# A pooling mixer on one Trainium2 core: the band in fp32 on its nonzero columns, seven warm-ups, one weight split on GpSimd, the scale in two transfers

## The chip, the cores and the metric

The kernel runs on one core of one Trainium2 chip. The metric is device microseconds (us) for one execution of the whole program. The engines are named as in the profile: PE (TensorE matmul) and PEld (its weight load), DVE (VectorE), ACT (ScalarE), POOL (GpSimd), SP (SyncE, which only issues transfers here). L351 is line 351 of the kernel before; L333 and the like, where said so, are lines of the changed kernel.

## The reference

Two decoder layers on x of 512 tokens by 1024 features in fp32. Layer 0 mixes tokens by a causal pooling, layer 1 by differential attention; after each mixer comes a LayerNorm on ALPHA * x + mixer(x), then a SwiGLU block with a second LayerNorm. Only the first mixer matters here. The features fall into four groups of 256; group g replaces each token by the mean of the last w tokens (w = 2, 4, 8, 16) less the token itself, multiplies by its own 256 x 256 weight and scales the result:

```python
pooled.append((hi - lo) / cnt)            # mean over the window, fewer tokens at the start
mixed = jnp.einsum('bsgc,gcd->bsgd', pooled - xg, w)
return mixed.reshape(B, S, D) * scale
```

As a matrix, "mean less itself" is a band: token t takes 1/w from each of tokens t-w+1 to t, less 1 at t. For a block of 128 tokens that act as sources only 144 columns of the band are nonzero: its own 128 tokens and the first 16 of the next block.

## The kernel before

All products that need fp32 accuracy are made of three products of a cheaper type, fp32r: each operand is split into a high part (rounded by ACT, L105) and a low part (the rest, subtracted by DVE, L106), and high x high, high x low and low x high are added (`mm3`, L123 to L125). Weights come from one tensor in pieces of 128 x 1024 (`fetch`, L95, issued by SP into five buffers `raw`), and are split by `ready` (L106). The order of instructions on each engine is the order in which the code is written; nothing is rescheduled. Each engine runs its own list in that order and waits where an operand isn't there.

The pooling stage is the head of the program. SP issues, in order, blocks 0 and 1 of x (`res`, L82), the first pooling weight `raw0`, the scale (L252, one row of 1024 values copied to all 128 partitions), block 2, the second pooling weight `raw1`, block 3, and gate weights from `raw2` on. Meanwhile POOL makes index ramps and the identity and fills the empty columns of the band tiles `fh` and `bh` with zeros (L276 to L278), DVE makes the band (L293 to L299), and ACT rounds a 16 x 16 corner `d0` for the first tokens, whose mean has fewer terms. PE runs 22 fp32 products of zeros (L312, `WARM`), whose result is used by nobody.

Each 128 x 512 half of a block of x is then split (`split_x`, eight times in all: blocks 0 and 1 ahead of the first pooled half, block 2 and block 3 later). `low` (L351 to L356) and `high` (L365, L366) multiply the split x with the band over 256 columns, zeros included, into eight PSUM banks `pool0_g` (tokens 0 to 255) and `pool1_g` (tokens 256 to 511). `scale_weights` multiplies a pooling weight by the scale on DVE (L325); `pool_weights` splits it (ACT L334, DVE L337); `split_pooled` splits a pooled bank; `mixed(s, d)` multiplies block s of the pooled tokens with the weights of two groups (24 products for both halves d). Then, block by block, DVE adds the result to x (`residual`, L154), takes statistics (L161, L167, L169), POOL takes the root (L170), DVE normalizes (L179), PE transposes (L206), ACT applies gain and shift (L225), and ACT and DVE split the result into `xt`, the input of the SwiGLU block. That block begins with tokens 0 to 255 alone: its first product, g<-xt,w2h, needs `xt` of blocks 0 and 1 and the split gate weight w2. Blocks 2 and 3 are turned between its first products. `w2` and `w3` are the first two gate weights (`raw2`, `raw3`); the low part of w2 is subtracted on DVE behind `spread_of(0, 0)`.

Of the kernel before, what the change touches and what calls it, by code (L numbers as in the profile page):

```python
# [11 lines left out]
F32 = mybir.dt.float32  # L12
F32R = mybir.dt.float32r
# [28 lines left out]
WARM = 22  # L42
# [10 lines left out]
def trunk(ctx, tc, x, wall, pscale, lam_p, subln, table, lng, lnb, first, onehot, out):  # L53
# [190 lines left out]
    with tc.tile_pool(name="pool", bufs=1) as pp:  # L244
# [4 lines left out]
        load_x(1)  # L249
        fetch(1)  # L250
        scale = pp.tile([P, D], F32, name="scale")
        nc.sync.dma_start(out=scale, in_=pscale.broadcast_to([P, D]))  # L252
        load_x(2)
        fetch(2)
# [3 lines left out]
        fh = pp.tile([P, 4, 256], F32R, name="fh")  # L258
        fl = pp.tile([P, 4, 256], F32R, name="fl")
        bh = pp.tile([P, 4, 512], F32R, name="bh")  # L260
        still = pp.tile([P, P], F32, name="still")
        nc.vector.memset(still, 0.0)
        nc.scalar.copy(
            fl.rearrange("p g (a t) -> p (g a) t", a=2), still.unsqueeze(1).to_broadcast([P, 8, P])
        )
# [10 lines left out]
        nc.gpsimd.memset(fh[:, :, 144:].bitcast(F32), 0.0)  # L276
        nc.gpsimd.memset(bh[:, :, 0:P].bitcast(F32), 0.0)
        nc.gpsimd.memset(bh[:, :, P + 144 :].bitcast(F32), 0.0)  # L278
# [12 lines left out]
        near = pp.tile([P, 4, 144], F32, name="near")  # L291
        for g, w in enumerate(WINDOWS):
            nc.vector.tensor_scalar(  # L293
                near[:, g, :], after, scalar1=float(w), scalar2=1.0 / w, op0=ALU.is_lt, op1=ALU.mult
            )
        own = ident.unsqueeze(1).to_broadcast([P, 4, P])
        for t in (fh[:, :, 0:144], bh[:, :, P : P + 144]):
            nc.vector.tensor_copy(t[:, :, P:], near[:, :, P:])
            nc.vector.tensor_tensor(t[:, :, :P], near[:, :, :P], own, op=ALU.subtract)  # L299
        xnh, xnl = (  # L300
            xt[:, i].rearrange("p a k s -> p (a k s)").rearrange("p (s d) -> p s d", s=SB)
            for i in range(2)
        )

        def split_x(s, d, low=None):
            c = slice(d * 512, (d + 1) * 512)
            split(xnh[:, s, c], xnl[:, s, c], res[:, s, c], low=low)
# [5 lines left out]
        split(fh[:16, :, 0:16], fl[:16, :, 0:16], d0)  # L313
        split_x(0, 0)
        split_x(0, 1)
        split_x(1, 0)
        split_x(1, 1)
# [25 lines left out]
        def xk(t, s, k):  # L343
            return t[:, s, k * P : (k + 1) * P]

        def low(t, ks):
            for k in ks:
                g = k // 2
                o = made[0, g][:, (k % 2) * 256 : (k % 2 + 1) * 256]
                if t == 0:  # L350
                    mm(o, xk(xnh, 0, k), fh[:, g, :], start=k % 2 == 0, stop=False)  # L351
                    mm(o, xk(xnh, 0, k), fl[:, g, :], start=False, stop=False)
                    mm(o, xk(xnl, 0, k), fh[:, g, :], start=False, stop=False)
                else:
                    mm(o, xk(xnh, 1, k), bh[:, g, 0:256], start=False, stop=False)
                    mm(o, xk(xnl, 1, k), bh[:, g, 0:256], start=False, stop=k % 2 == 1)  # L356

        def high(blocks, ks):
            for s in blocks:
                c = (3 - s) * P  # L360
                for k in ks:
                    g = k // 2
                    o = made[1, g][:, (k % 2) * 256 : (k % 2 + 1) * 256]
                    b = bh[:, g, c : c + 256]
                    mm(o, xk(xnh, s, k), b, start=s == 1 and k % 2 == 0, stop=False)  # L365
                    mm(o, xk(xnl, s, k), b, start=False, stop=s == 3 and k % 2 == 1)  # L366
# [1053 lines left out]
```

## Time and profile before

| | us |
|---|---|
| median of 3 runs (lowest, highest) | 946.09 (945.66, 946.59) |
| the profiled execution | 946.19 |
| its span, first to last instruction | 944.4 |
| PE busy in the span | 932.3 (99%) |
| DVE busy in the span | 823.5 (87%) |
| start of the first gate product, g<-xt,w2h | 36.70 |

The span begins with the first instruction that the profile shows; 1.79 us of the profiled execution lie outside it. A timeline row gives the start, the duration, the engine, the line and the operation, what it writes and reads, and how many such instructions were merged; in brackets stands how long its engine had been idle and what it waited for. A matmul of PE starts before the one ahead of it has drained, so its pace is the distance between starts, not its duration. One fp32 product is two PE instructions (22 warm-ups are 44), one fp32r product is one.

### The profile page before, as it was taken

The numbers are of one execution on the slowest core, as the hardware profiler recorded it, in microseconds if no ns is written. First come the engines' busy times: TensorE is split into PE (matmuls) and PEld (weight loads), VectorE is DVE, ScalarE is ACT, GpSimd is POOL, SyncE is SP. The second block draws the span as 40 slices with busy tenths as digits, with TensorE's granted clock in tenths as the row PEclk, the third lists the DMA queues.
The fourth block names the chain that finished last, engine by engine and source line by source line (L and its number), as shares of the span: only waits on it lengthen the run. The fifth ranks groups of instructions, "written<-read, shape, count | busy, mean of one in ns | idle before, by whom it ended". The sixth has DMA issues, their size and how long they took to land. (4 is left out here: it accounts for less than half of the span.)

```text
span 944.4 us, 16089 instructions
## 1 busy us (share of the span) xinstructions
PE 932.3 (99%) x6293; PEld 858.9 (91%) x6293; DVE 823.5 (87%) x1220; ACT 505.8 (54%) x810; POOL 104.9 (11%) x136
## 2 busy tenths in 40 slices
PE   9999999999999999999999999999999999999996
PEld 9899999999988888988888888899999999988885
DVE  7999999999988798688777676799999999988898
ACT  5664454554564467665556553844455554663550
POOL 2111121110001101000000000211111110001101
PEclk9999999999999999999999999999999999999998
DMA  7288998886878965432232232389998786878962
GB/s 272 70 254 271 300 291 260 253 264 205 259 243 269 357 211 157 148 90 101 67 91 78 67 90 90 100 250 276 277 283 252 246 272 211 257 235 274 360 223 89
DMA packets 73499, 197.40 MB, mean 209 GB/s; under 512 B 6546, under 2 KB 17970, under 8 KB 73424
## 3 DMA queue, kind: packets, MB, share of 16 engines
q1 hardware_dynamic: 33840, 114.44, 36.8%
q0 software_dynamic: 15952, 47.31, 18.5%
q10 hardware_dynamic: 23632, 34.63, 9.9%
q8 instruction: 49, 0.80, 0.3%
q14 instruction: 26, 0.21, 0.1%
HBM read 159.64 MB, written 36.72 MB: 208 GB/s over the span
## 5 line engine op out<-in xcount | busy, mean ns | idle before, releaser
L603 DVE TENSOR_TENSOR raw<-raw,raw 128x1024 f32<-128x1024 f32 x72 | 87.8, 1219 | 0.6
L105 ACT CAST xs<-hid 128x512 fp32r<-128x512 f32 (+1 forms) x60 | 34.7, 582 | 28.5 <-DVE hid L768 28.5
L106 DVE TENSOR_TENSOR xs<-hid,xs 128x512 fp32r<-128x512 f32 (+1 forms) x60 | 38.3, 640 | 7.8 <-ACT xs L105 7.8
L225 ACT ACTIVATE y<-pt,gbT 128x128 f32<-128x128 f32 x92 | 34.6, 456 | 19.3 <-PE pt L206 19.3
L1142 ACT ACTIVATE p<-p,mn 128x128 f32<-128x128 f32 (+3 forms) x64 | 35.4, 554 | 14.9 <-DVE mn L1137 14.9
L699 POOL DMA_DIRECT2D b<-in_wall x24 | 17.9, 793 | 155.4 <-DMA tsum<-b 132.4
L760 POOL DMA_DIRECT2D xs<-ssum x24 | 17.4, 725 | 141.8 <-PE Q L915 119.3
L170 POOL TENSOR_TENSOR rs<-rs,mhalf 128x1 f32<-128x1 f32 x16 | 12.6, 791 | 167.8 <-DVE rs L169 167.8
L875 ACT ACTIVATE sg<-sg 128x512 f32<-128x512 f32 x18 | 11.4, 633 | 33.5 <-DVE sg L866 33.5
L1137 DVE CUSTOM_DVE_ANT_0 p<-s,bias 128x128 f32<-128x128 f32 (+3 forms) x64 | 28.1, 485 | 0.0
L106 POOL TENSOR_TENSOR sql<-sq,sqh 128x512 fp32r<-128x512 f32 x7 | 9.1, 1294 | 165.3 <-ACT sqh L105 165.3
L736 ACT CAST v<-u 128x512 fp32r<-128x512 f32 x22 | 13.7, 621 | 22.1 <-DVE u L734 22.0
L106 DVE TENSOR_TENSOR xt<-y,xt 128x512 fp32r<-128x512 f32 x23 | 15.5, 686 | 11.4 <-ACT xt L105 11.4
L699 POOL DMA_DIRECT2D hid<-in_wall x20 | 14.7, 734 | 95.2 <-DMA tsum<-hid 71.7
L858 ACT COPY hid<-C 128x512 f32<-128x512 f32 x18 | 10.6, 588 | 24.2 <-PE C L847 24.2
L161 DVE BATCH_NORM_STATS2 st<-res 128x6 f32<-128x512 f32 x32 | 22.2, 694 | 1.1
L106 DVE TENSOR_TENSOR heads<-k,heads 128x512 fp32r<-128x512 f32 x8 | 5.5, 691 | 20.2 <-ACT heads L105 20.2
L862 DVE TENSOR_TENSOR hid<-C,hid 128x512 f32<-128x512 f32 x18 | 12.4, 690 | 10.9 <-PE C L847 9.2
L700 POOL DMA_DIRECT2D b<-in_wall x12 | 14.8, 1229 | 57.1 <-DMA b<-in_wall 47.2
L105 ACT CAST heads<-k 128x512 fp32r<-128x512 f32 x8 | 4.7, 588 | 26.3 <-PE k L125 26.3
L1156 DVE SCALAR_TENSOR_TENSOR p<-p,sm,p 128x128 f32<-128x128 f32 (+3 forms) x32 | 17.6, 551 | 1.1
L1132 PE MATMUL s<-heads 64*128 64x256 f32 (+2 forms) x192 | 17.9, 330 | 0.0
(1150 smaller groups left out, 3804.7 us busy)
## 6 DMA issues: line engine op xcount, KB each, us to landing
raw<-in_wall SPq DMA_DIRECT2D x122, 512.0 KB, 4.2
r<-tsum SPq DMA_DIRECT2D x40, 512.0 KB, 4.4
b<-in_wall POOLq DMA_DIRECT2D x36, 512.0 KB, 5.9
hid<-in_wall POOLq DMA_DIRECT2D x30, 512.0 KB, 6.0
r<-in_wall SPq DMA_DIRECT2D x30, 512.0 KB, 5.0
tsum<-b ACTq DMA_DIRECT2D x24, 512.0 KB, 5.1
ssum<-v ACTq DMA_DIRECT2D x22, 512.0 KB, 3.6
tsum<-hid ACTq DMA_DIRECT2D x20, 512.0 KB, 5.0
```

What stands on the lines that cost most here:

```text
L105: nc.scalar.copy(dst_h, src)
L106: (low or nc.vector).tensor_tensor(dst_l, src, dst_h.bitcast(F32), op=ALU.subtract)
L161: nc.vector.bn_stats(stats[n, s][:, d, :], res[:, s, d * 512 : (d + 1) * 512])
L225: nc.scalar.activation(y[:, k, :], src, AF.Identity, bias=b, scale=g)
L603: tt(t, raws[pair[0]], raws[pair[1]], op=ALU.add)
L699: nc.gpsimd.dma_start(out=t[:, j], in_=src[:, j])
L700: nc.gpsimd.dma_start(out=t[:, 0], in_=src[:, :, 1], accum_op=ALU.add)
L760: nc.gpsimd.dma_start(out=t.bitcast(F32), in_=ssum[:, 0 if p == "P7" else 1, :, r, :])
L1132: nc.tensor.matmul(accs[c][:, :wide], a[r, qs], b[r, :wide], start=i == 0, stop=i == 2)
L1137: nc.vector.tensor_tensor_reduce(out=p, in0=accs[c][:, :w], in1=biases[h][:, w - 1 :: -1] if w < S else biases[h][:, ::-1], op0=ALU.add, o ...
L1142: nc.scalar.activation(p, p, AF.Exp, bias=mn[:, q, c : c + 1], scale=-1.0, accum_out=sm[:, q, c : c + 1],)
L1156: nc.vector.scalar_tensor_tensor(p0[:, r], p0[:, r], sm[:, q, 0:1], p1[:, r], op0=ALU.mult, op1=ALU.add)
```

## The change

The band is applied to x as it is, in fp32: `split_x`, `low` and `high` go, and `shares` takes their place. It multiplies a 128 x 128 piece of a block of x with only those columns of the band that are not zero (144, 128 or 16), in one fp32 product each. The tiles `fh`, `fl` and `bh` give way to `band` and `edge` (the band with the corner `d0` for the first block), 144 columns wide, without zero columns to fill. The warm-ups are 7 instead of 22. The scale comes in two transfers of 512 columns, the first ahead of `raw0`, the second behind block 2. The low part of w2 is subtracted on POOL. The code behind it stands in a somewhat other order: the split of the second half of the pooled tokens now follows both residuals of block 1, and the split of w3 is made in one piece.

```diff
-WARM = 22
+WARM = 7
...
+        load_scale(0)
         fetch(1)
-        scale = pp.tile([P, D], F32, name="scale")
-        nc.sync.dma_start(out=scale, in_=pscale.broadcast_to([P, D]))
         load_x(2)
+        load_scale(1)
         fetch(2)
...
-        nc.gpsimd.memset(fh[:, :, 144:].bitcast(F32), 0.0)
-        nc.gpsimd.memset(bh[:, :, 0:P].bitcast(F32), 0.0)
-        nc.gpsimd.memset(bh[:, :, P + 144 :].bitcast(F32), 0.0)
...
+        nc.scalar.copy(edge[:, :, P:], band[:, :, P:])
         own = ident.unsqueeze(1).to_broadcast([P, 4, P])
+        for t in (edge, band):
+            nc.vector.tensor_tensor(t[:, :, :P], band[:, :, :P], own, op=ALU.subtract)
+        nc.scalar.copy(edge[:16, :, 0:16], d0)
...
-        split(fh[:16, :, 0:16], fl[:16, :, 0:16], d0)
-        split_x(0, 0)
-        split_x(0, 1)
-        split_x(1, 0)
-        split_x(1, 1)
...
+        def shares(half, s, source, a, b, o, first=False):
+            for k in range(KB):
                 g = k // 2
+                c = (k % 2) * 256 + o
+                mm(
+                    made[half, g][:, c : c + b - a],
+                    res[:, s, k * P : (k + 1) * P],
+                    source[:, g, a:b],
+                    start=first and k % 2 == 0,
+                    stop=False,
+                    skip_group_check=True,
+                )
...
-        low(0, range(4))
-        low(0, range(4, 8))
-        low(1, range(8))
+        shares(0, 0, edge, 0, 144, 0, True)
+        shares(0, 1, band, 0, P, P)
+        shares(1, 1, band, P, 144, 0, True)
         scale_weights(0)
-        high((1,), range(8))
         pool_weights(0)
         split_pooled(0, 0, 1)
+        shares(1, 2, band, 0, 144, 0)
         mixed(0, 0)
-        split_x(2, 0)
-        split_x(2, 1)
-        high((2,), range(8))
         scale_weights(1)
...
-        split_x(3, 0)
-        split_x(3, 1)
-        summed(0, 0)
...
+        ready(3, nc.gpsimd)
+        mixed(1, 1)
+        shares(1, 3, band, 0, P, P)
+        summed(0, 0, 1)
+        spread_of(0, 0)
...
-        high((3,), range(8))
...
+        summed(1, 0)
+        norm(0, 0)
+        summed(1, 1)
+        spread_of(0, 1)
+        split_pooled(1, 0, 1)
+        norm(0, 1)
```

On DVE, between the split of the pooled bank of group 1 and the first residual, the kernel before has these rows (`pooled` is the split pooled tile, `xt<-res` a split of x, `raw_88` the second pooling weight, `pw1l` its low part, `mix_0` the first product of block 0):

```order
L106 TENSOR_TENSOR pooled<-pool_1_131,pooled 128x2x256 [waits Activation_49]
L106 TENSOR_TENSOR xt<-res,xt 128x512 [waits DMAHW5_49,Activation_49]
L106 TENSOR_TENSOR xt<-res,xt 128x512 [waits Activation_49]
L325 TENSOR_TENSOR raw_88<-raw_88,scale 128x512 [waits DMAHW6_49]
L325 TENSOR_TENSOR raw_88<-raw_88,scale 128x512
L106 TENSOR_TENSOR pooled<-pool_2_132,pooled 128x2x256 [waits Activation_49]
L106 TENSOR_TENSOR pooled<-pool_3_133,pooled 128x2x256 [waits Activation_49]
L337 TENSOR_TENSOR pw1l<-raw_88,pw1h 128x512 [waits Activation_49] x2
L106 TENSOR_TENSOR xt<-res,xt 128x512 [waits DMAHW7_49,Activation_49]
L106 TENSOR_TENSOR xt<-res,xt 128x512 [waits Activation_49]
L154 SCALAR_TENSOR_TENSOR res<-res,mix_0_236 128x512 [waits PE_49]
```

On the same engine at the same place the changed kernel has (`raw_89` is now the second pooling weight, L311 its scaling, L323 its low part):

```order
L106 TENSOR_TENSOR pooled<-pool_1_126,pooled 128x2x256 [waits Activation_49]
L311 TENSOR_TENSOR raw_89<-raw_89,scale 128x512 [waits DMAHW7_49,DMAHW6_49]
L311 TENSOR_TENSOR raw_89<-raw_89,scale 128x512
L106 TENSOR_TENSOR pooled<-pool_2_127,pooled 128x2x256 [waits Activation_49]
L106 TENSOR_TENSOR pooled<-pool_3_128,pooled 128x2x256 [waits Activation_49]
L323 TENSOR_TENSOR pw1l<-raw_89,pw1h 128x512 [waits Activation_49] x2
L106 TENSOR_TENSOR tbl<-tb,tbh 33x8 [waits DMASW2_49,Activation_49]
L154 SCALAR_TENSOR_TENSOR res<-res,mix_0_182 128x512 [waits DMAHW0_49,PE_49]
```

The four splits of x are gone; the scaling now waits for two transfers, its weight and the second half of the scale.

Further down on DVE, from the statistics of block 0 to the split of the second pooled half, the kernel before has (`mv` and `rs` hold mean and inverse root, `w2l` is the low part of the first gate weight, `mix_0_282` and `mix_1_283` the two halves of block 1):

```order
L169 TENSOR_SCALAR rs_0_347<-mv_0_345 128x1 [waits DVE_49]
L106 TENSOR_TENSOR w2l<-raw_91,w2h 128x1024 [waits DMAHW0_49,Activation_49]
L106 TENSOR_TENSOR tbl<-tb,tbh 33x8 [waits DMASW2_49,Activation_49]
L154 SCALAR_TENSOR_TENSOR res<-res,mix_0_282 128x512
L161 BN_STATS st_1_377<-res 128x6 [waits DVE_49]
L179 TENSOR_SCALAR res<-res,mv_0_345,rs_0_347 128x1024 [waits Pool_49]
L106 TENSOR_TENSOR pooled<-pool_0_134,pooled 128x2x256 [waits PE_49,Activation_49]
```

And the changed kernel, from the same row on (`mix_0_208` and `mix_1_209` are block 1):

```order
L169 TENSOR_SCALAR rs_0_281<-mv_0_279 128x1 [waits DVE_49]
L154 SCALAR_TENSOR_TENSOR res<-res,mix_0_208 128x512 [waits DMAHW2_49]
L161 BN_STATS st_1_285<-res 128x6 [waits DVE_49]
L179 TENSOR_SCALAR res<-res,mv_0_279,rs_0_281 128x1024 [waits Pool_49]
L154 SCALAR_TENSOR_TENSOR res<-res,mix_1_209 128x512 [waits PE_49]
L161 BN_STATS st_1_285<-res 128x6 [waits DVE_49]
L167 BN_AGGR mv_1_290<-st_1_285 128x2 [waits DVE_49]
L169 TENSOR_SCALAR rs_1_292<-mv_1_290 128x1 [waits DVE_49]
L106 TENSOR_TENSOR pooled<-pool_0_129,pooled 128x2x256 [waits Activation_49]
```

The low part of w2 has left DVE, and the second residual of block 1 with its statistics now stands ahead of the pooled split instead of behind it.

On POOL the subtraction of w2 is now queued ahead of the roots; the changed kernel's rows from its last transfers of constants on are:

```order
L285 DMA tb<-in_table 32x8 [waits Pool_49]
L287 DMA oh__113<-in_onehot 33x640
L106 TENSOR_TENSOR w2l<-raw_92,w2h 128x1024 [waits DMAHW1_49,Activation_49]
L170 TENSOR_TENSOR rs_0_281<-rs_0_281,mhalf 128x1 [waits DVE_49]
L170 TENSOR_TENSOR rs_1_292<-rs_1_292,mhalf 128x1 [waits DVE_49]
```

In the kernel before, the first root follows `oh_` directly.

72 lines of the change are left out of this document (12 added, 60 removed).

## The prediction

> **What bounds the kernel now.** First the page's shares of busy time, then busy time by stage: the stage of the change ends at 36.70, where the first gate product starts.
>
> ```profile
> PE 932.3 (99%) x6293; PEld 858.9 (91%) x6293; DVE 823.5 (87%) x1220; ACT 505.8 (54%) x810; POOL 104.9 (11%) x136
> core 0: us, PE busy (x) PEld busy (x) DVE busy (x) ACT busy (x) POOL busy (x), PEclk, DMA share, GB/s
> 0.00:36.70 36.70, 33.83 (x250) 33.05 (x250) 31.52 (x60) 23.98 (x45) 7.54 (x20) 0.95 0.56 204
> 36.70:67.00 30.30, 30.30 (x256) 30.30 (x255) 28.68 (x36) 19.71 (x36) 6.55 (x8) 1.00 0.67 191
> ```
>
> From 36.70 on PE never stops, so an earlier start of that product is worth its whole shift, if what feeds PE moves along. Before it, PE's 33.83 us say little: they hold warm-ups and a stretch at half clock. PE's rows show where that stage is held:
>
> ```profile
> 1.06 5.65 PE L312 MATMUL pool<-still 128*128 128x128 f32 x25 [1.06 <-DVE still L262]
> 6.34 2.37 PE L312 MATMUL pool<-still 128*128 128x128 f32 x19
> 8.58 0.36 PE L351 MATMUL pool<-fh,xt 128*128 128x256 f32 x1
> 26.84 1.81 PE L206 MATMUL pt<-ident,res 128*128 128x128 f32 x8 [1.82 <-DVE res L179]
> 28.30 0.56 PE L123 MATMUL mix<-pw0h,pooled 128*128 128x256 f32 x1
> 36.02 0.39 PE L439 MATMUL line<-ohr,tbh 33*8 33x512 f32 x1
> 36.70 0.39 PE L123 MATMUL g<-xt,w2h 128*128 128x256 f32 x1
> ```
>
> PE waits once, 1.82 us for DVE's normalization. DVE is the engine to follow; these are the rows that carry it:
>
> ```profile
> 5.12 2.57 DVE L106 TENSOR_TENSOR xt<-res,xt 128x512 fp32r<-128x512 f32 x4 [0.75 <-ACT xt L105]
> 8.98 1.29 DVE L325 TENSOR_TENSOR raw<-raw,scale 128x512 f32<-128x512 f32 x2 [1.29 <-DMA scale<-in_pscale]
> 13.98 1.28 DVE L106 TENSOR_TENSOR xt<-res,xt 128x512 fp32r<-128x512 f32 x2
> 15.19 1.29 DVE L325 TENSOR_TENSOR raw<-raw,scale 128x512 f32<-128x512 f32 x2
> 18.79 1.28 DVE L106 TENSOR_TENSOR xt<-res,xt 128x512 fp32r<-128x512 f32 x2
> 20.00 0.68 DVE L154 SCALAR_TENSOR_TENSOR res<-res,mix 128x512 f32<-128x512 f32 x1
> 21.59 0.69 DVE L154 SCALAR_TENSOR_TENSOR res<-res,mix 128x512 f32<-128x512 f32 x1 [0.19 <-PE mix L125]
> 23.28 0.15 DVE L169 TENSOR_SCALAR rs<-mv 128x1 f32<-128x1 f32 x1
> 23.36 1.22 DVE L106 TENSOR_TENSOR w2l<-raw,w2h 128x1024 fp32r<-128x1024 f32 x1
> 24.51 0.15 DVE L106 TENSOR_TENSOR tbl<-tb,tbh 33x8 fp32r<-33x8 f32 x1
> 25.90 0.80 DVE L179 TENSOR_SCALAR res<-res,mv,rs 128x1024 f32<-128x1024 f32 x1
> 35.88 0.69 DVE L106 TENSOR_TENSOR xt<-second,xt 128x512 fp32r<-128x512 f32 x1
> ```
>
> A row without a bracket didn't wait. From 13.98 to the last row the only wait shown is 0.19 us; that row, the low part of the last piece of `xt`, ends at 36.57 and the gate product starts at 36.70. That chain is what an edit must shorten; PE's own chain, up to the same point, is nearly as long.
>
> **The change part by part.**
>
> *Warm-ups and the first shares.* The 25 warm-up instructions to 6.34 take 5.28 us, 0.211 each; the 19 behind them 2.24 us, 0.118 each. So the 14 that are left end at about 4.0. The first share needs block 0 of x and the corner; the first cast of before shows when x is there:
>
> ```profile
> 4.47 2.42 ACT L105 CAST xt<-res 128x512 fp32r<-128x512 f32 x4 [0.34 <-DMA res<-in_x]
> L312 PEld LDWEIGHTS pool<-still 128*128 128x128 f32 x44 | 7.6, 273 | 1.1 <-DVE still L262 1.1
> ```
>
> PE's pool work thus starts at 4.45 instead of 8.58. No row has this product on real x; the warm-up is the same form. Priced by it, 144 columns are 16 instructions of 0.211 x 1.125 while slow and 0.118 x 1.125 when fast: shares(0,0) is 2.1 to 3.8, and with the pace doubling near 6.4 as before it ends at about 7.5; shares(0,1) adds 1.9 (9.4). For 16 columns the bounds are an eighth of that (0.24) and all of it (1.9), since the weight load stays whole; I take 1.2, nearer the load (10.6). shares(1,2) ends at 12.7. Fast, the five come to 9.2 us. Before, 88 fp32r products did this; PE's pace from 36.70 on is 256 instructions in 30.30 us, 0.118 each, so they were 10.4: fp32 costs PE nothing.
>
> *First pooling weight and the scale.* Here are the issues and, in the same order, the times to landing of raw0, scale, raw1, raw2, and the rate at which data moved:
>
> ```profile
> 1.66 0.42 SPq L95 DMA_DIRECT2D raw<-in_wall  x1
> 2.12 0.43 SPq L252 DMA_DIRECT2D scale<-in_pscale  x1
> 3.26 0.45 SPq L95 DMA_DIRECT2D raw<-in_wall  x1
> 4.47 45.50 SPq L95 DMA_DIRECT2D raw<-in_wall  x10
> raw<-in_wall SPq DMA_DIRECT2D x1, 512.0 KB, 5.3
> scale<-in_pscale SPq DMA_DIRECT2D x1, 512.0 KB, 6.8
> raw<-in_wall SPq DMA_DIRECT2D x1, 512.0 KB, 9.4
> raw<-in_wall SPq DMA_DIRECT2D x1, 512.0 KB, 10.7
> 9.00:10.00 1.00, 1.00 (x11) 1.00 1.00 390
> ```
>
> raw0 landed at 6.96, scale at 8.92, raw1 at 12.66, raw2 at 15.2. With 256 KB less ahead of them raw0 and the first half of the scale land 0.65 us earlier, at 8.3. Two scalings (1.2), a cast (0.6, ACT is free), two low parts, two pooled splits take DVE to 12.1. The second scaling then needs raw1, which has the same bytes ahead as before: 12.7, the extra issue (0.43) being hidden, as later transfers wait for the bytes ahead anyway (raw2: issued at 4.47, landed at 15.2). So raw1 is late next, and the second scaling moves from 15.19 to 12.7: 2.5 earlier (the split of block 2, 13.98 to 15.19, lies within this).
>
> *From there DVE has no slack*, so each removed row counts at its pitch: the split of block 3, 18.79 to 20.00, 1.21; w2l, 23.36 to 24.51, 1.15; the wait of 0.19 for PE, whose products behind shares(1,2) end at 12.7 + 3 x 1.4 and a short wait for the second weight, near 17.2, half a us before DVE asks. Sum 2.5 + 1.21 + 1.15 + 0.19 = 5.05: the last xt row ends at 36.57 - 5.05 = 31.5.
>
> *w2l on POOL.* The rows for it:
>
> ```profile
> L106 POOL TENSOR_TENSOR sql<-sq,sqh 128x512 fp32r<-128x512 f32 x7 | 9.1, 1294 | 165.3 <-ACT sqh L105 165.3
> 23.52 1.49 POOL L170 TENSOR_TENSOR rs<-rs,mhalf 128x1 f32<-128x1 f32 x1 [17.25 <-DVE rs L169]
> 29.72 0.56 POOL L170 TENSOR_TENSOR rs<-rs,mhalf 128x1 f32<-128x1 f32 x1 [4.71 <-DVE rs L169]
> ```
>
> Twice the columns is 2.6 us. raw2 lands at 15.2, ACT rounds by 16.4 (two of the casts that took 2.42 for four, 1.2), POOL is done at 19.0. Queued behind it is block 0's root, whose input is ready at 23.28 + 0.15 - 2.5 - 1.21 - 0.19 = 19.5: 0.5 us of cover. The gate product needs w2l only at the end. If that cover went, the normalization would wait.
>
> The first root took 1.49 us where the second took 0.56: it started 0.16 us into DVE's subtraction of w2, ran on to 25.01, and w2l ended at 24.58. The Trainium skill, "SBUF — State Buffer", section "Who interferes with whom", says why: a DVE instruction with two SBUF inputs and a GpSimd instruction that reads SBUF shut each other out, and the later one waits in full. By that rule POOL's long subtraction can hold DVE, which speaks against this move; in my times DVE then does residuals with an operand in PSUM, and the sum stays.
>
> *PE's tail.* In the new order DVE, after the first normalization (25.90 - 5.05 = 20.85), 0.7 long, does a residual and statistics (1.4) and their spread (0.5) before the first pooled split (0.7), which ends at 24.1. PE, after the next 12 products and shares(1,3) at about 20.5, waits to 21.7, does 8 transposes (0.8, the 28.30 - 26.84 above being at half clock) and waits again to 24.1. From there it has 46 products of 0.12, 8 transposes and the bias lines (36.70 - 36.02): 7.0 us, to 31.1, hidden under DVE's 31.5, if the clock is whole. It was not in before:
>
> ```profile
> 26.00:27.00 1.00, 0.16 (x2) 1.00 0.83 307
> 27.00:28.00 1.00, 1.00 (x6) 0.50 0.40 160
> 30.00:31.00 1.00, 1.00 (x9) 0.80 0.00 0
> ```
>
> After 1.82 us of idleness PE had half its clock from 27.0 to 30.4, 3.4 us. Now there are two gaps, 1.2 and 1.6 us, within 3.6. I take one such stretch again: bounds 0 and 1.7 (half of 3.4), and 1.4 as some of it falls into waiting. PE is then the later one: 31.1 + 1.4 = 32.5.
>
> *The rest at nothing:* eight casts less on ACT, which is not the later one at any step above; three memsets less on POOL, whose small transfers (0.115 MB, 0.3 us at 390 GB/s) come earlier and stay ahead of raw1 as before. If ACT became the later one, a cast is 0.6.
>
> *Sum.* The gate product starts at 32.5 instead of 36.70, 4.2 earlier; DVE is then further ahead than before, so nothing behind it gives this back. Span 944.4 - 4.2 = 940.2; the profiled execution lies 1.8 above its span, so **942.0**. That execution (946.19) stands 0.1 above the median of 946.09, which changes nothing.
>
> **The rivals.**
>
> 1. *The clock stays whole* through PE's two gaps, each shorter than 1.82. Then DVE ends the stage at 31.5: 5.2 earlier, 941.0. Against it: together the gaps leave PE idle in 2.8 of 3.6 us. The Trainium skill, "TensorE: Matmul & The Clock Gate", section "Why this matters for your kernels", puts the limit at idle gaps of about 3 us, so by that rule this is what happens; the 1.82 us above contradict it.
> 2. *The two halves of the scale are slow.* The whole took 8.92 - 6.96 = 1.96 us where its neighbours took about 1.3; if each half takes as long as the whole, raw1 lands up to 1.96 later, at 14.6, and the gain falls to 2.2: 944.0.
> 3. *POOL and DVE shut each other out*: w2l starts late and the root, or DVE's pw1l and normalization, wait up to its 2.6 us. Gain 1.6: 944.6.
> 4. *Slower: the clock doesn't rise.* 14 instructions and a gap of 0.4 may not be taken for steady work. At half clock the five shares and the first 36 products run from 4.45 to 26.5 (3.8 + 3.4 + 2.4 + 3.8, then 36 x 0.238), 4.9 after their end before; less 1.15 for w2l, 3.8 late: 950.0. It decides if the pace hasn't doubled by about 12. Against it: in before it doubled at 6.34 after 5.3 us of the same work. The Trainium skill, same page and section, asks for 4 us or more of warming up ahead of measured matmuls; by that rule seven, 3.0 us, are too few.
> 5. *Given back later*: something in the gate products was nearly late. Then 946.2. Against it stands DVE's lead.
>
> **How the numbers follow.** Forecast 44%, rival 1 24%, rival 2 16%, rival 3 7%, rival 4 6%, rival 5 3%. The likeliest gives 942.0. Low end: rival 1 and 0.7 more, should raw1 land at the pace of its faster neighbours (1.3 instead of 1.9): 940.3. High end: rival 2 at its worst and 0.3 of the 0.5 by which a run lies above the median: 944.3. Left out are 4, 5, most of 3. About 0.2%, 1.9 us, is what a measurement of this kernel can tell from no change, so faster means under 944.2: the forecast, rival 1, 13 of rival 2's 16 and 1 of rival 3, 82%; within it 6 of rival 3, 3 of 2 and all of 5, 12%; slower rival 4, 6%.
>
> **What would show it.** First share near 4.5; the first scaling near 8.3, the second at 12.7 and waiting for a transfer; no idle DVE from there on; POOL's subtraction over before the first root; a half-clock stretch between 23 and 28; the gate product at 32.5. Wrong would be: a pace of 0.2 beyond 10 us, a root of more than 1 us, a gate product after 34.8, or a shift that shrinks behind it.

## The result, and the profile after

The changed kernel takes 942.11 us (median of 10 runs, 941.27 to 944.93) beside 946.11 for the kernel before on the same chips (10 runs). The ratio is 0.9959, with a 95% interval of 0.9948 to 0.9970: 4 us faster. A second set of six runs, below, gave 0.9967 (0.9955 to 0.9978), 3 us.

The execution that was profiled is the slowest of the ten: 944.93, span 943.1, only 1.3 less than the span before. So this trace shows more losses than most runs have, and the first task is to find them. Busy time by stage, as for the kernel before; the gate product now starts at 34.23:

```profile
core 0: us, PE busy (x) PEld busy (x) DVE busy (x) ACT busy (x) POOL busy (x), PEclk, DMA share, GB/s
0.00:34.23 34.23, 31.09 (x211) 29.75 (x211) 25.82 (x50) 19.74 (x38) 7.13 (x18) 0.90 0.61 219
34.23:67.00 32.77, 32.77 (x276) 32.77 (x275) 30.21 (x37) 19.21 (x34) 7.30 (x9) 1.00 0.68 192
```

DVE's work ahead of that product fell from 31.52 to 25.82 us, 5.7 less, but the product moved only 2.47 (36.70 to 34.23). The mean clock of the stage is 0.90; it was 0.95. PE's rows in the new head:

```profile
1.06 3.35 PE L303 MATMUL pool<-still 128*128 128x128 f32 x14 [1.06 <-DVE still L265]
4.50 2.56 PE L333 MATMUL pool<-edge,res 128*128 128x144 f32 x16
6.90 3.64 PE L333 MATMUL pool<-band,res 128*128 128x128 f32 x32
10.94 3.15 PE L333 MATMUL pool<-band,res 128*128 128x144 f32 x16 [0.40 <-DMA res<-in_x]
23.14 1.06 PE L206 MATMUL pt<-ident,res 128*128 128x128 f32 x8 [0.64 <-DVE res L179]
25.40 0.38 PE L125 MATMUL mix<-pw0h,pooled 128*128 128x256 f32 x1 [0.96 <-DVE pooled L106]
34.23 0.39 PE L123 MATMUL g<-xt,w2h 128*128 128x256 f32 x1
```

The first share starts at 4.50 as forecast. The third row holds shares(0,1), 128 columns wide, and the 16-column shares of block 1. The three gaps (0.40, 0.64, 0.96 us) are shorter than the one of 1.82 before, and yet the clock fell twice; in these rows the number behind PE's busy time is the granted clock:

```profile
12.00:13.00 1.00, 1.00 (x7) 0.54 1.02 410
15.00:16.00 1.00, 1.00 (x8) 0.75 1.05 418
25.00:26.00 1.00, 0.60 (x4) 0.87 0.00 0
29.00:30.00 1.00, 1.00 (x10) 0.93 0.02 8
```

Between the first two and between the last two of these rows it stood at 0.50: half clock from 12.1 to 15.5 and from 25.7 to 29.1 (worked out from the four means). The second stretch was forecast, the first was not. DVE:

```profile
9.12 1.29 DVE L311 TENSOR_TENSOR raw<-raw,scale 128x512 f32<-128x512 f32 x2 [5.32 <-DMA raw<-in_wall]
12.91 1.28 DVE L311 TENSOR_TENSOR raw<-raw,scale 128x512 f32<-128x512 f32 x2
19.11 0.69 DVE L154 SCALAR_TENSOR_TENSOR res<-res,mix 128x512 f32<-128x512 f32 x1 [1.12 <-PE mix L125]
32.26 0.69 DVE L106 TENSOR_TENSOR xt<-second,xt 128x512 fp32r<-128x512 f32 x1
```

The first scaling waits for its weight until 9.12, not 8.3; the second doesn't wait. At 19.11 stands the price of the first half-clock stretch: PE's mixes are late and DVE, which should not have waited any more, waits 1.12 us. The last `xt` row ends at 32.95, and PE is the later one, as forecast. POOL did what it was given, with no harm to the root behind it (0.57 us where the first root before took 1.49):

```profile
16.61 2.43 POOL L106 TENSOR_TENSOR w2l<-raw,w2h 128x1024 fp32r<-128x1024 f32 x1 [12.25 <-ACT w2h L105]
21.04 0.57 POOL L170 TENSOR_TENSOR rs<-rs,mhalf 128x1 f32<-128x1 f32 x1 [2.00 <-DVE rs L169]
```

So 2.47 us were won at the head. PE keeps them to its last product (935.91 before, 933.48 after), but the span shrinks by 1.3 only. The rest is lost in the last layer, where DVE subtracts low parts of weight blocks that are read back from DRAM (`d_24` and on), then adds the last products and normalizes. Two DVE rows of before,

```profile
884.33 1.21 DVE L106 TENSOR_TENSOR d_24l<-r,d_24h 128x1024 fp32r<-128x1024 f32 x1
920.69 0.69 DVE L902 SCALAR_TENSOR_TENSOR res<-res,P 128x512 f32<-128x512 f32 x1 [0.42 <-PE P L915]
```

and the same two after:

```profile
883.36 1.23 DVE L106 TENSOR_TENSOR d_24l<-r,d_24h 128x1024 fp32r<-128x1024 f32 x1 [1.37 <-ACT d_24h L105]
919.46 0.68 DVE L864 SCALAR_TENSOR_TENSOR res<-res,P 128x512 f32<-128x512 f32 x1
```

Before, `d_24l` found its operand ready, and at 920.69 DVE still waited for PE: it had caught up. After, it waited 1.37 us for `d_24`, whose read-back came late, and 36 us further it is still behind: no wait at 919.46. From the last product's start to the end of the span are 8.49 us before and 9.62 after; the difference, 1.13, is what was given back.

### The profile page after: what moved, and what is told of

It is laid out like the page before. It is cut to its first block, busy times and chain, and to the rows that moved or that the text cites. A ratio compares the mean times of both kernels' runs of the same rounds, so it can differ in the third digit from the quotient of the medians.

```text
span 943.1 us, 15993 instructions
## 1 busy us (share of the span) xinstructions
PE 929.6 (99%) x6255; PEld 855.5 (91%) x6255; DVE 817.1 (87%) x1208; ACT 500.8 (53%) x802; POOL 104.6 (11%) x134
## 5 line engine op out<-in xcount | busy, mean ns | idle before, releaser
L106 DVE TENSOR_TENSOR xt<-y,xt 128x512 fp32r<-128x512 f32 x23 | 15.5, 687 | 12.4 <-ACT xt L105 12.4
L820 ACT COPY hid<-C 128x512 f32<-128x512 f32 x18 | 10.6, 588 | 24.1 <-PE C L809 24.0
L662 POOL DMA_DIRECT2D b<-in_wall x12 | 14.8, 1229 | 56.2 <-DMA b<-in_wall 50.5
```

The costliest lines, as they stand in the source:

```text
L106: (low or nc.vector).tensor_tensor(dst_l, src, dst_h.bitcast(F32), op=ALU.subtract)
L662: nc.gpsimd.dma_start(out=t[:, 0], in_=src[:, :, 1], accum_op=ALU.add)
```

## The experiments

Two theories came out of this. *Head*: the gate product's start is set by two chains that meet, DVE's (first weight, scalings, residuals) and PE's (warm-ups, shares, mixes, at the clock it is granted). *Tail*: part of what the head wins is lost when a read-back of the last layer lands late. All times are medians; the ratio to the kernel before on the same chip stands beside them with its interval. Line numbers are each kernel's own.

### 1. The same kernel again

> The kernel after, unchanged, for a second profiled execution and ten more times. Clock theory: the executions differ because TensorE falls to half clock for a stretch of 3.4 us a different number of times before 35 us (twice in the first profile: 12.0 to 15.4 and 25.9 to 29.3); then the median is 942.1 again with a spread of 941.3 to 945, and in the profile the gate product's start (34.23 in the first) and the span move together: at 32.3 to 33.2 if a stretch is missing. Tail theory: the executions differ because in the first profile VectorE ran 1.2 us late behind the last layer's read-backs (d_24 to d_27, around 885); then the start of the gate product is the same 34.2 and the last rows differ. DVE theory (my forecast): gate product at 32.5 whatever the clock did.

943.15 (941.23 to 943.91), 0.9967. The profiled execution (942.56, span 940.8) has one half-clock stretch, 24.4 to 27.9; PE's rows and two clock rows:

```profile
21.97 1.06 PE L206 MATMUL pt<-ident,res 128*128 128x128 f32 x8 [0.86 <-DVE res L179]
24.23 0.43 PE L125 MATMUL mix<-pw0h,pooled 128*128 128x256 f32 x1 [0.96 <-DVE pooled L106]
33.06 0.39 PE L123 MATMUL g<-xt,w2h 128*128 128x256 f32 x1
24.00:25.00 1.00, 0.77 (x4) 0.72 0.00 0
27.00:28.00 1.00, 1.00 (x8) 0.57 0.00 0
```

The same instructions gave the gate product at 34.23 with two stretches and at 33.06 with one. A third execution of the same head, in experiment 9 (which changes nothing before 885), had none:

```profile
21.77 1.06 PE L206 MATMUL pt<-ident,res 128*128 128x128 f32 x8 [0.87 <-DVE res L179]
24.04 0.39 PE L125 MATMUL mix<-pw0h,pooled 128*128 128x256 f32 x1 [0.96 <-DVE pooled L106]
31.43 0.39 PE L123 MATMUL g<-xt,w2h 128*128 128x256 f32 x1
```

The gaps in the second and third are the same to 0.01 us, and yet one execution has a stretch and the other has none. From the second gap's end to the gate product are 8.83 us with a stretch (the first profile, 1 and 6) and 7.39 without (2, 5, 7 and 9), so one costs 1.44 here.

The clock records in the traces show part of what decides it. In every trace kept here the changes of the clock lie whole multiples of 3.41 us apart; in the first profile it is full from 5.25, half from 12.08, full from 15.49, half from 25.73 and full from 29.15. So they keep to a beat of 3.41 us, and the beat lies at another place of the program in each run: the first rise is at 3.96 in experiment 1, at 5.25 in the first profile and at 6.04 in experiment 9. Here are the beat of the first profile that holds both gaps, and the two beats of experiment 9 that divide them between each other:

```profile
22.32:25.73 3.41, 1.81 (x13) 1.00 0.00 0
19.69:23.11 3.42, 2.52 (x21) 1.00 0.52 163
23.11:26.52 3.41, 2.48 (x20) 1.00 0.00 0
```

Where one beat held both gaps, PE was busy in 1.60 to 1.81 of its 3.41 us, and the clock fell at its end (the first profile, 1 and 6); so it did in the kernel before, whose one gap lay within a beat with 1.59 us busy. Where a beat ended between the gaps, with 2.46 to 2.54 us busy on each side, it stayed whole (7 and 9). That isn't the whole rule: experiments 2, 8 and 12 have beats with 1.83, 1.57 and 1.55 us busy and no fall behind them.

Both theories hold a part: the scatter begins at the head, and in this execution nothing was lost at the tail (8.49 us behind the last product's start, DVE waiting 0.49 for PE at 917.09).

### 2. The 16-column shares made wide

```diff
-band = pp.tile([P, 4, 144], F32, name="band")
+band = pp.tile([P, 4, 256], F32, name="band")
+nc.gpsimd.memset(band[:, :, 144:], 0.0)
...
-shares(1, 1, band, P, 144, 0, True)
+shares(1, 1, band, P, 256, 0, True)
```

> The eight 16-column products of block 1 on the second half are made 128 columns wide with zero columns of the band; the result is the same. Clock theory: the 16-column products leave TensorE counted as idle, so the stretch of half clock at 12.0 to 15.4 goes, the mixes start at a pace of 0.12 instead of 0.21, VectorE's wait of 1.12 us for the mix of block 1 goes: median 941.2, slowest runs 1 us lower. Rival, the 16-column products are cheap and the stretch comes from the wait for the third block of x (0.40 us at 10.9): the wide ones take 1 us more on TensorE ahead of that block's products, the stretch stays: 942.1 to 943. Third: they take as long as 128 columns already and the clock doesn't depend on them: 942.1.

942.40 (941.32 to 943.28), 0.9960 (0.9947 to 0.9972): no difference that can be told. The profiled execution has no stretch and the gate product at 31.54, yet a span of 940.6, as its tail lost 1.0 (9.53). None of the five profiled executions with wide shares in this place (2, 4, 10, 11, 12) fell to half clock near 12; of the six with narrow ones and seven warm-ups, three did (the first profile, 3, 5), three didn't (1, 7, 9). That leans towards the narrow products as a cause and doesn't show it: in 2, 4 and 11 the wide products also leave no wait for block 2 of x, the expectation's rival cause, and the place of the beat differs from run to run. (The mix that DVE waited 1.12 us for is the second half of block 0, not block 1 as the expectation has it.)

### 3 and 4. Products of zeros in PE's gaps

Experiment 3 is the kernel after with twenty such products, 4 the one with wide shares and the same twenty.

```diff
+def busy(t, n):
+    for _ in range(n):
+        mm(t[:, 0:P], still, still, start=True, stop=True)
...
-transposed(0, 0)
-mixed(2, 0)
-transposed(0, 1)
+transposed(0, 0, lambda t: busy(t, 7))
+mixed(2, 0, first=lambda t: busy(t, 9))
+transposed(0, 1, lambda t: busy(t, 2))
...
-mixed(2, 1)
+mixed(2, 1, first=lambda t: busy(t, 2))
```

> Twenty fp32 products of the zero block, whose results are overwritten, stand in TensorE's four gaps between 22 and 29 us (7 ahead of the transposes of block 0, 9 ahead of the first mix of block 2, 2 and 2 ahead of the next two groups). Clock theory: no stretch of half clock between 22 and 30, the gate product starts about 1.2 us earlier (33.0 where the first profile had 34.23): median 940.9. Rival, VectorE sets the end of the stage and TensorE's pace is hidden behind it: 942.1. Third, the added products stand in the way of ready work: 942.5 to 943.5, and the row of the first mix of block 2 starts later than 25.4.

> The wide products and the twenty added ones together. Clock theory: full clock from the first rise to the last products, the gate product at 32.3 to 32.8, all executions within 0.6 us of each other, median 940.2. Rival (VectorE bound, or the scatter comes from the last layer): median 941 to 942.1 with the same spread of 3 us as the kernel after.

944.30, 0.9978 (0.9969 to 0.9987), and 943.38, 0.9977 (0.9967 to 0.9987): slower than the kernel after by 1 us and more by the ratios. The clock fell once in 3, from 11.0 to 14.4, ahead of the added products, and was whole from there on; in 4 it was whole throughout, as the clock theory has it. But the gate product started at 35.28 and 33.78. Two rows of experiment 4 say why:

```profile
20.95 1.83 PE L378 MATMUL pt<-still 128*128 128x128 f32 x14
23.49 2.17 PE L378 MATMUL mix<-still 128*128 128x128 f32 x18
```

Seven products are 14 instructions, 1.83 us, where the idle time is 0.9. I had priced a product by one instruction; the filling was twice as long as the gaps, and with PE's chain as long as DVE's every product too many is late work.

### 10. Five products instead of twenty

As 4, with two products ahead of the transposes and three ahead of the mix.

> The wide products and five added fp32 products of the zero block (two ahead of the transposes of block 0, three ahead of the first mix of block 2; each is two instructions of 0.12 us, so 0.5 and 0.7 us in idle time of 0.6 and 1.0 us). Clock theory: full clock to the gate product at 31.6 to 32.2 in every execution, median 941.3, slowest below 942.8. Rival, the gain at the head is given back in the last layer whatever the clock: median 941.8 to 942.8 with the same spread. Third, the added products still hold up ready work as the twenty did: gate product later than 33, 943 or more.

942.31 (941.13 to 943.08), 0.9957 (0.9946 to 0.9969). Now they fit:

```profile
21.04 0.71 PE L378 MATMUL pt<-still 128*128 128x128 f32 x4
22.82 0.83 PE L378 MATMUL mix<-still 128*128 128x128 f32 x6
24.25 0.38 PE L125 MATMUL mix<-pw0h,pooled 128*128 128x256 f32 x1 [0.36 <-DVE pooled L106]
31.64 0.39 PE L123 MATMUL g<-xt,w2h 128*128 128x256 f32 x1
```

Full clock, no loss at the tail (8.48), span 939.5, time 941.29: that is the end of the scale that the kernel after reaches by itself in its fastest runs (941.27, span 939.5). The median is no lower than the kernel after's 942.11. The tail's scatter, which a whole clock at the head leaves as it is, would explain that; the other runs have no profile to show it. The clock theory's price for the head holds (gate product 31.64), its median of 941.3 does not. Neither this nor any other version here beats the kernel after by more than the intervals.

### 5. The low part of w2 back on DVE

```diff
-ready(3, nc.gpsimd)
+ready(3)
```

> The kernel after with the first gate weight's low part back on VectorE, at the same place of the program. DVE theory (my forecast's term of 1.15 us): it stands in VectorE's queue ahead of the residual sums of block 0 and everything behind it is 1.1 us later where TensorE's clock is whole: median 943.2 to 944.2, the gate product 1.1 us later than in a kernel after with the same stretches of half clock. Clock theory: where the mixes run at half clock VectorE waits 1.12 us for the mix of block 1 anyway and the product hides in it; then the median moves by less than 0.6 us. Third, Pool's subtraction costs VectorE time beside it (shared access), so that taking it away gives back some: below 942.1.

943.73 (942.40 to 946.02), 0.9977 (0.9968 to 0.9987): 0.9 to 1.7 us worse than the two sets of the kernel after by the ratios, with intervals that overlap at their ends or more. The rows:

```profile
16.41 1.21 DVE L106 TENSOR_TENSOR w2l<-raw,w2h 128x1024 fp32r<-128x1024 f32 x1
17.55 0.67 DVE L154 SCALAR_TENSOR_TENSOR res<-res,mix 128x512 f32<-128x512 f32 x1
```

The residual starts at 17.55 where the kernel after has it at 16.44 to 16.64, and 1.14 behind the start of the subtraction, so the 1.15 us of the forecast is there. The gate product is at 32.65, 1.22 later than in experiment 9; neither has a stretch behind its second gap. The subtraction also hid in part in this execution, as the second expectation said it could: a stretch at half clock (11.3 to 14.8) cost DVE no wait, since the subtraction stood where the wait of 1.12 us had been.

### 6. The warm-ups back to 22

```diff
-WARM = 7
+WARM = 22
```

> The kernel after with 22 warm-ups in place of 7. PE theory: the first shares start about 2.7 us later (4.7 to 7.4), the pooled block is split 1 to 2 us later, the gate product follows: median 943.6. DVE theory: the first split of the pooled block at 11.7 waits for VectorE's first scaling (9.1, waiting for a transfer) and the third block of x holds TensorE until 11 anyway, so at most 0.4 us comes out at the end: 942.1 to 942.6. Third, the longer warm-up keeps the clock whole through 12 to 15: below 942.

945.26 (943.94 to 946.97), 0.9993 (0.9985 to 1.0002): almost the whole gain is gone. PE's rows,

```profile
1.06 8.00 PE L303 MATMUL pool<-still 128*128 128x128 f32 x44 [1.06 <-DVE still L265]
8.89 2.13 PE L333 MATMUL pool<-edge,res 128*128 128x144 f32 x16
```

and two of DVE's:

```profile
18.02 0.69 DVE L154 SCALAR_TENSOR_TENSOR res<-res,mix 128x512 f32<-128x512 f32 x1 [0.94 <-PE mix L125]
20.90 0.69 DVE L154 SCALAR_TENSOR_TENSOR res<-res,mix 128x512 f32<-128x512 f32 x1 [1.47 <-PE mix L125]
```

The shares start 4.4 us later, and DVE waits for the mixes, 0.94 and 1.47. With one stretch (27.5 to 30.9) the gate product is at 36.02, 2.96 later than in experiment 1 with one. The PE theory holds, with more than it asked for.

### 7. The scale in one transfer

```diff
-load_scale(0)
 fetch(1)
+nc.sync.dma_start(out=scale, in_=pscale.broadcast_to([P, D]))
 load_x(2)
-load_scale(1)
 fetch(2)
```

> The kernel after with the scale in one transfer, issued behind the first weight as in the kernel before. DVE theory: the first scaling waits for the later of weight and scale either way, within 0.4 us of 9.1; the second block of scale is no longer behind the third block of x, which comes about 1 us later (TensorE's wait before its products grows from 0.4 to 0.7 us to 1.5): median 942.1 to 942.7. Rival, the split is what brought the first scaling forward: it goes to 10.3 or later, and the gate product with it: 943.3. Third: the narrow transfers are slow in themselves, and one is better: 941.5.

943.22 (942.19 to 944.10), 0.9971 (0.9960 to 0.9982): a ratio within the interval of the kernel after's second set and just outside that of its first, so not told apart by the time. At the head it is seen:

```profile
9.86 1.29 DVE L310 TENSOR_TENSOR raw<-raw,scale 128x512 f32<-128x512 f32 x2 [6.07 <-DMA scale<-in_pscale]
```

The first scaling starts 0.75 to 0.95 later than with two transfers (8.91 to 9.12) and now waits for the scale; with the clock whole the gate product is at 32.31 beside 31.43, 0.9 later. The first expectation named the cost too low (0.4), the second too high (1.2); PE's wait for block 2, which the first had at 1.5, was 0.42.

### 8. The side edits without the new shares

The kernel before with seven warm-ups, two scale transfers and w2's low part on POOL, and with its splits of x as they were.

```diff
-WARM = 22
+WARM = 7
...
+load_scale(0)
 fetch(1)
-scale = pp.tile([P, D], F32, name="scale")
-nc.sync.dma_start(out=scale, in_=pscale.broadcast_to([P, D]))
 load_x(2)
+load_scale(1)
...
-ready(3)
+ready(3, nc.gpsimd)
```

> The kernel before with the three side edits (seven warm-ups, scale in two transfers, the first gate weight's low part on Pool) but with its splits of x and the band in three partial products. If VectorE's five splits of x are what the gain rests on (2.5 + 1.2 of 4.2 us in the forecast), this gives the 1.15 us of the low part and little else: 944.5 to 945. Rival, the side edits carry it: 942 to 943. Third, they do nothing without the other: 945.8 to 946.1.

946.19 (944.97 to 947.22), 0.9999 (0.9991 to 1.0008): nothing, as the third expectation had it. Its gate product is at 35.60, 1.10 earlier than in the kernel before; but that execution had a stretch at half clock in PE's tail and this one has none, and in the changed kernel one costs 1.44. Part of the reason is the clock at the start: after seven warm-ups and a stop of 0.67 us PE goes on at 0.21 us per product, and the pace doubles only at this row, 24 products later, so that DVE waits 0.44 us at its first pooled split:

```profile
10.62 0.31 PE L361 MATMUL pool<-bh,xt 128*128 128x256 f32 x1
```

Another is a new wait. POOL's row and DVE's:

```profile
23.09 2.38 POOL L106 TENSOR_TENSOR w2l<-raw,w2h 128x1024 fp32r<-128x1024 f32 x1
```

```profile
23.78 2.24 DVE L179 TENSOR_SCALAR res<-res,mv,rs 128x1024 f32<-128x1024 f32 x1
```

In the order of the kernel before, POOL's subtraction falls on block 0's normalization, which takes 2.24 us instead of 0.80. In the order of the kernel after it lies ahead of the first root. The placement made that edit work, not the engine alone. So this run leaves out two things at once, the new shares and the new order; no run has the shares in the old order, and what the order is worth alone stays open.

### 9 and 11. Two low parts of the last layer on POOL

Experiment 9 is the kernel after with this edit, 11 is experiment 10 with it.

```diff
-split(h, l, drops.pop(j))
+split(h, l, drops.pop(j), low=nc.gpsimd if final and j in (38, 40) else None)
```

> The kernel after with the low parts of two of the last layer's read-back blocks (d_38 and d_40, 1.13 us each on VectorE) taken by Pool; nothing before 885 changes. Tail theory: in the last 25 us the end is set by VectorE's queue, 1.1 us of it behind a late read-back in some executions; two low parts less take up to 2.2 us off its end, until the last product (2 us ahead of the last sum in an execution without the delay, 5 us ahead in the one of the wide products) becomes the later one: median 940.6 to 941.4, spread smaller than the 3 us of the kernel after. Head theory (only TensorE's start of the gate product decides): no change, 942.1 to 943.2. Third, Pool's 2.4 us for such a product makes TensorE wait for d_38 or d_40, or slows VectorE beside it: 943.5 or more.

> The wide products, the five added ones, and the two low parts on Pool. If head and tail are both as described, the gate product starts at 31.6 to 32.2 and VectorE's queue at the end no longer holds it: median 939.5 to 940, all executions within 1.5 us. If only the tail counts: as the kernel with the two low parts on Pool alone, within 0.3 us. If Pool's subtraction costs more than it brings: 942 or more.

943.99 (940.64 to 948.15), 0.9978 (0.9965 to 0.9992), and 942.41 (940.71 to 944.71), 0.9963 (0.9949 to 0.9978). Their best runs are the fastest of all (940.64, span 938.9), but 9's worst is more than 2 us slower than the kernel before's median. In 9's profiled execution, the best of its set, DVE gets so far ahead that it waits for PE's last sum, which it adds at 931.39 instead of 932.04 in experiment 10, with the head alike:

```profile
910.76 2.56 POOL L106 TENSOR_TENSOR d_38l<-r,d_38h 128x1024 fp32r<-128x1024 f32 x1 [8.85 <-ACT d_38h L105]
911.23 2.64 DVE L106 TENSOR_TENSOR xs<-hid,xs 128x512 fp32r<-128x512 f32 x1 [0.20 <-ACT xs L105]
931.39 0.69 DVE L864 SCALAR_TENSOR_TENSOR res<-res,P 128x512 f32<-128x512 f32 x1 [0.36 <-PE P L877]
```

Already there DVE's subtraction beside POOL's takes 2.64 instead of 0.68. In 11's profiled execution (944.71), whose read-backs issued from 874 on took 9.6 us to land (the median) where those of 9 took 5.5, the two stand on each other longer, and PE waits for what DVE owes it:

```profile
911.82 4.73 POOL L106 TENSOR_TENSOR d_38l<-r,d_38h 128x1024 fp32r<-128x1024 f32 x1 [7.27 <-ACT d_38h L105]
914.33 3.30 DVE L106 TENSOR_TENSOR d_39l<-r,d_39h 128x1024 fp32r<-128x1024 f32 x1
923.76 0.73 PE L886 MATMUL P<-d_39h,xs 128*128 128x512 f32 x2 [1.48 <-DVE xs L106]
```

So DVE's queue does set the end, as the tail theory says, and the third expectation is right as well: taking work off it in this way costs more than it brings where the read-back is late, as far as these two profiles show.

### 12. The first weight ahead of the second block of x

Experiment 10 with one load moved.

```diff
-load_x(1)
 scale = pp.tile([P, D], F32, name="scale")
...
 load_scale(0)
 fetch(1)
+load_x(1)
 load_x(2)
```

> The kernel with the wide and the five added products, with the first half of the scale and the first weight loaded ahead of the second block of x. VectorE theory: the first scaling, for whose weight VectorE sits idle until 9.2, starts at 7.9 to 8.2, the first split of the pooled block then waits for TensorE's shares of the second block of x (it lands 1.3 us later) until 11.0 to 11.4, and the gate product starts 0.4 to 0.9 us earlier than 31.64: 30.8 to 31.2. In the time, the last layer gives part back: median 941.3 to 942.3. Rival, TensorE's shares now set the first split of the pooled block: gate product at 31.6 or later, 942.3 to 943. Third, what is gained at the head comes out whole: 941.0 to 941.5.

944.67 (943.27 to 945.92), 0.9976 (0.9965 to 0.9986), worse than all three theories had it. The first scaling does start at 7.95. But PE stands still, and so does what needs it:

```profile
9.93 2.25 PE L336 MATMUL pool<-band,res 128*128 128x128 f32 x18 [3.12 <-DMA res<-in_x]
```

```profile
11.27 1.29 DVE L106 TENSOR_TENSOR pooled<-pool,pooled 128x512 fp32r<-128x512 f32 x2 [0.65 <-ACT pooled L105]
12.98 1.29 DVE L314 TENSOR_TENSOR raw<-raw,scale 128x512 f32<-128x512 f32 x2 [0.43 <-DMA raw<-in_wall]
```

PE waits 3.12 us for block 1 of x, its mixes are late, and the gate product starts at 33.72, 2.1 later. DVE gained 0.5 at the first split of the pooled tokens (11.27 beside 11.77 in experiment 10) and lost it at the second scaling, where the second weight is now the late one. The trace shows one thing more: the clock stayed whole across the 3.12 us in which PE stood still, its longest gap in the heads of all these runs.

## Why the prediction came out

**The number.** 942.0 was forecast, with 941.0 for a whole clock; 942.11 and 943.15 were measured. The execution with the one stretch that the forecast assumes (experiment 1) has the gate product at 33.06 and span 940.8 where 32.5 and 940.2 were forecast. That the median agrees to 0.1 us is luck in part: faster executions (941.27, span 939.5) and slower ones (up to 944.93) lie on both sides of it, and the second set's median is 1 us higher.

**Warm-ups and first share**: right. 4.48 to 4.67 for 4.45, and the clock rose in time: the 32 instructions from 6.90 take 3.64 us, 0.114 each, so rival 4 is out for this kernel. With the old products behind the same seven warm-ups (experiment 8) its mechanism is there: half clock until 10.6. What the forecast didn't see is how much this edit carries: undone, it takes 2.96 us of head with it (experiment 6).

**The shares' price**: mis-sized. Shares(0,1) and the 16-column shares start at 6.90 and take 3.64 us; 128 columns alone take 1.95 (block 3's, at 20.35 in this trace), so the narrow ones take about 1.7, near the upper bound of 1.9 and not the 1.2 taken. Nothing waited for it but the next product, which waited for block 2 of x anyway.

**First scaling 8.3, raw1 late next**: this step failed. The weight landed at 9.1, 0.8 late: while the first half of the scale moves, 5.00 to 7.00, the trace has 147 and 201 GB/s, where 390 was assumed (rival 2's mechanism, in the half that stands ahead of the weight). One transfer instead of two would have made it 9.86 (experiment 7). The second scaling then started at 12.91, without a wait: raw1 landed at 12.7, as forecast (issued at 3.57, 9.1 to landing), but DVE, 0.8 late at the first scaling, came to it 0.2 after that. In experiment 12, with DVE earlier, the second scaling does wait for it, until 12.98. So the end of that step (12.7) is right to 0.2 and its reason is wrong.

**From there no slack, each row at its pitch**: right where the clock is whole. In experiment 9 the last `xt` row ends at 31.57, forecast 31.5, and the low part of w2 is worth its 1.15 (experiment 5). But the gate product there starts at 31.43, ahead of that row's end and 7.39 behind PE's second gap: PE sets it even with the clock whole, where the forecast had PE hidden under DVE. In the first profile a half-clock stretch at 12.1, which the forecast did not have, put 1.12 us of waiting into it.

**w2l on POOL**: right; 2.43 us for 2.6, over at 19.04 for 19.0, root of 0.57. Rival 3 didn't happen here, and experiments 8, 9 and 11 show what its price is where the two engines do meet. The Trainium skill, "SBUF — State Buffer", section "Who interferes with whom", says that a DVE instruction with two SBUF inputs and a GpSimd instruction that reads SBUF exclude each other and whoever comes second waits in full; the 2.64 and 3.30 us of DVE and the 4.73 of POOL agree. The normalization of 2.24 us has one tensor operand and two scalars and isn't the case of that sentence, yet it too ends only behind POOL's subtraction (26.02 and 25.47 in experiment 8).

**PE's tail and the clock**: the size is right, the certainty was wrong. A stretch costs 1.44 (1.4 forecast), and the way from the second gap to the gate product without one is 7.39 (7.0 counted). The gaps were mis-sized, 0.64 to 0.87 and 0.96 us for 1.2 and 1.6. And there is not "one such stretch again": the same head had two, one and none in three executions, with gaps alike to 0.01 us in two of them. The Trainium skill, "TensorE: Matmul & The Clock Gate", section "Why this matters for your kernels", warns of idle gaps beyond about 3 us; here the clock fell with no gap above 0.96, and stayed whole across one of 3.12 (experiment 12). That rival 1 is one outcome of the same program, and not another theory of it, is what the forecast missed. Where the beat of 3.41 us lies in a run tells the stretches of experiments 1 and 6 and of the first profile from their absence in 7 and 9; how much of a beat PE must be idle is not shown, and experiment 2, with both gaps in one beat, had no stretch.

**Nothing behind it gives this back**: wrong in some executions, rival 5 in small, and with it a sign that the forecast had named as its own, a shift that shrinks behind the gate product. From the last product's start to the end are 8.46 to 8.55 us in the kernel before and in experiments 1, 5, 7, 10 and 12, and 8.89 to 10.08 in the first profile and in 2, 3, 4, 6 and 8 (9 and 11, whose last layer was changed, are left out). That experiments 6 and 8, with late heads, have it too says that it isn't caused by being early. In the first profile it starts with the read-backs issued from 874 on; their median from issue to landing is 9.0 us, 6.7 in experiment 1, with the DMA engines busy in nine tenths of the time in both. Why they are late in one execution and not in another stays open.

**Where the gain comes from.** Neither part has it alone: the side edits without the shares and the new order give 0.9999, the shares and the order without fewer warm-ups 0.9993, all together 0.9959. Two chains lead to the residuals of block 0, and each edit shortens one. Two splits of x, 1.2 us each, stood in DVE's behind the first pooled split: with them its first residual is at 19.15 (experiment 8), without at 16.44 to 16.64. The warm-ups stood in PE's: with 22 of them the second residual waits for its mix until 20.90 (experiment 6), with seven it is at 17.96 (experiment 1). With both short they are in balance: moving one load in favour of one (experiment 12) costs 2 us on the other.

## What to carry to other kernels

Where two engines' chains meet, price an edit on both: a saving on one is worth only as much as the other allows, and two sets of edits that each measure nothing can be worth 4 us together. An edit of a few us is to be judged over many executions and with the profile of more than one: here the same instructions spread over 3.7 us, and the single trace at hand was the slowest. Work moved to POOL paid where DVE beside it had an operand in PSUM or was waiting, and stretched both engines where both subtracted in SBUF; it stretched a normalization as well.

## What the runs showed of the hardware

- The clock changed only at whole multiples of 3.41 us from its other changes, on a beat that lay elsewhere in each run. It halved for one beat behind gaps of 0.86 and 0.96 us, or didn't, in the same program; with the first gap filled and 0.36 us left of the second it stayed whole (experiment 10), and it stayed whole across a single gap of 3.12 us (experiment 12).
- An fp32 product of 16 columns takes about 0.11 us per instruction, one of 128 columns 0.12: narrow fp32 products save next to nothing on PE.
- The first half of the scale, a row of 512 values copied to 128 partitions, moved at 147 to 201 GB/s where plain loads before and after it moved at 401 and 418. The second half, which moved along with the end of block 2, wasn't as slow (280 and 363 GB/s from 9 to 11).
- A normalization (one tensor operand and two scalars) took 2.24 us beside a POOL subtraction, 0.80 without it.
